# First norm of a one-layer encoder kernel taken from turned tokens, its first couple of weights in program order, and the rests of splits emitted one step later

## The chip, the cores and the metric

The kernel runs on one core of a Trainium2 chip. The metric is the time of one execution in microseconds (us) of the device, as a median of three runs; lower is better. TensorE (PE in the rows) multiplies matrices, VectorE (DVE) and ScalarE (ACT) work on elements, GpSimd (POOL) is hardly used, and the queue of SyncE (SP) issues all transfers.

## The reference, cut to what matters

```python
def swiglu(x, w_gate, w_up, w_down):
    return (silu(x @ w_gate) * (x @ w_up)) @ w_down

h = h + 0.5 * swiglu(rms_norm(h, norm_ffn1), ffn1_gate, ffn1_up, ffn1_down)
u = rms_norm(h, norm_mix)
xc, bg, cg, q, k, v, g_conv, g_attn = split(u @ w_in)
...                                   # gated convolution, differential attention, w_o
h = h + 0.5 * swiglu(rms_norm(h, norm_ffn2), ffn2_gate, ffn2_up, ffn2_down)
out = rms_norm(h, norm_final)
```

There are 1024 tokens of 1024 features; the hidden width of a swiglu is 2816. All is float32. `rms_norm` divides each token by the root of its mean square and multiplies by a gain for each feature.

## The kernel before, in words

**Layout.** Features lie on the 128 partitions and tokens along the row, so that x is `h[o][t]`: o is the half of the features (four blocks of 128), t the half of the tokens (512). A tile `Q` holds such a quarter, or 1 MB of weights; there are 19 of them. `C` is a tile of 128x512, `A` and `F` are tiles of 128x2x4x128 for stationary operands.

**Precision.** A float32 product is made of three matmuls of a rounded type: each operand is split into `hi`, a rounded copy made by ScalarE, and `lo = src - hi`, made by VectorE; then hi·hi, hi·lo and lo·hi are summed in PSUM. A group of one stationary tile and one quarter is 12 matmuls of 128x512.

**Fast product.** The weights of a swiglu come in pairs of 256 columns of gate and of up; the first pair is number 0. A product of a pair with x is a 2x2 product of blocks, done by seven products of sums of blocks (`ORDER`, `A_STEPS`, `B_STEPS`) in place of eight. The seven sums of quarters of x (`Blocks`, split into hi and lo) are made once and used by ten pairs; the sums of weights are made for each pair. A pair has 14 groups: seven of gate, seven of up. `submit` prepares a job's stationary operand, and runs the job four submits later. Pair 0 is done by eight plain products, since the seven sums aren't ready yet.

**Order.** Most of the program is ordered by a scheduler. The start (class `Start`) stands in the order of its code on TensorE, VectorE and ScalarE.

**The start before.** Pair 0 is multiplied with x times the gain, not yet divided by the root, in 16 groups; the results are multiplied with the root afterwards (`ev`). For the root, `squares` squares 16 tiles of 128x512 on ScalarE and VectorE adds them up (`add_square`); `norm` sums over partitions with a matmul against ones and makes the root in full width (`rstd`). `apply` then multiplies each quarter by gain and root in place, and the seven sums are made of that. The operands of the second half of the tokens are split twice: once without the root for pair 0 (`operand`), once with it for the later pairs.

**PSUM.** Tag `sc` has two buffers of 128x1024, `at` two, `ps` and `ot` one each of 128x512.

## Time and profile before

| | us |
|---|---|
| median of three runs | 2038.38 (2038.37 to 2039.26) |
| the profiled execution, its own time | 2041.61 |
| its span, first to last instruction | 2039.7 |
| TensorE busy | 1964.6 (96%) |
| VectorE busy | 1408.3 (69%) |
| ScalarE busy | 928.0 (45%) |
| mean granted clock of TensorE | 0.986 |

Busy TensorE of 96% says that over the whole span little is to be had anywhere but where TensorE waits. Such places are few: the first 100 us, and some stretches between 600 and 1450 us. In a row of a timeline, the number in square brackets is how long the engine was idle before it, with what ended that. A clock of 1.00 is 2.4 GHz, 0.50 is 1.2 GHz.

### The profile page before, as it was taken

How to read it: one execution, taken by the hardware profiler on the slowest of the kernel's cores; microseconds unless marked ns; L12 is line 12 of the kernel's file. 1: busy time of each engine (PE TensorE's matmuls, PEld its weight loads, DVE VectorE, ACT ScalarE, POOL GpSimd, SP SyncE). 2: the span in 40 equal slices, each digit the busy share in tenths (PEclk: the TensorE clock that was granted, in tenths of full speed). 3: DMA queues.
4: the chain of work that ended last, by engine and by line, in shares of the span. 5: the costliest groups of instructions: out<-in, count | busy, mean ns of one | idle time of the engine just before them, and what ended most of it. 6: DMA issues, size and time to landing. Idle time of an engine off the chain costs nothing.

```text
span 2039.7 us, 24072 instructions
## 1 busy us (share of the span) xinstructions
PE 1964.6 (96%) x8808; PEld 1617.4 (79%) x8808; DVE 1408.3 (69%) x2198; ACT 928.0 (45%) x1668; POOL 91.8 (4%) x91
## 2 busy tenths in 40 slices
PE   9799999999999999998999989999999999999997
PEld 7588888888887888886778867777788888888885
DVE  8976666666766755678576757988856656666874
ACT  6533333354355553233466645465433333353462
POOL 0000000000000000000344400000000000000000
PEclk9899999999999999999999999999999999999998
DMA  5132322345444332423424248032332232264341
GB/s 218 71 110 104 119 88 103 112 168 229 170 151 148 114 119 83 139 94 95 156 82 133 86 120 326 27 117 100 115 112 104 98 111 97 99 260 153 144 162 56
DMA packets 78582, 259.68 MB, mean 127 GB/s; under 512 B 9728, under 2 KB 16000, under 8 KB 60800
## 3 DMA queue, kind: packets, MB, share of 16 engines
q1 hardware_dynamic: 78464, 258.15, 35.3%
q8 instruction: 69, 1.13, 0.2%
q14 instruction: 49, 0.40, 0.1%
HBM read 183.14 MB, written 74.97 MB: 127 GB/s over the span
## 4 chain that ended last, share of the span: by engine, by line
PE 83%; DVE 11%; ACT 2%; issue 2%; DMA 1%; POOL 0%; SPq 0%; DVEq 0%; ACTq 0%; POOLq 0%
PE sc L273 37%; PE at L273 16%; PE ps L273 9%; PE ot L273 8%; DVE Q L249 3%; PE ps L1204 2%; PE sc L1265 1%; PE ps L1265 1%; DVE C L249 1%; DVE F L249 1%; PE at L1265 1%; PE sc L345 1%; PE sc L344 1%; PE sc L346 1%; PE sc L1000 1%
## 5 line engine op out<-in xcount | busy, mean ns | idle before, releaser
L273 PE MATMUL sc<-Q,A 128*128 128x512 f32 x2052 | 497.5, 392 | 13.8 <-DVE C L316 7.8
L273 PEld LDWEIGHTS sc<-Q,A 128*128 128x128 f32 x2052 | 388.2, 189 | 96.9 <-DVE C L316 8.1
L273 PE MATMUL sc<-Q,F 128*128 128x512 f32 x1488 | 362.6, 393 | 17.7 <-ACT Q L254 11.2
L273 PEld LDWEIGHTS sc<-Q,F 128*128 128x128 f32 x1488 | 281.7, 190 | 78.6 <-ACT Q L254 12.3
L249 DVE TENSOR_TENSOR F<-Q,F 128x512 fp32r<-128x512 f32 (+1 forms) x311 | 215.4, 697 | 170.9 <-ACT F L254 170.6
L249 DVE TENSOR_TENSOR Q<-Q,Q 128x512 fp32r<-128x512 f32 (+4 forms) x350 | 286.8, 873 | 34.4 <-ACT Q L254 27.1
L254 ACT CAST F<-Q 128x512 fp32r<-128x512 f32 (+1 forms) x319 | 193.7, 614 | 249.2 <-PE sc L273 88.5
L254 ACT CAST A<-Q 128x512 fp32r<-128x512 f32 (+1 forms) x303 | 183.9, 613 | 243.8 <-PE sc L273 100.9
L249 DVE TENSOR_TENSOR A<-Q,A 128x512 fp32r<-128x512 f32 (+1 forms) x303 | 205.1, 679 | 122.4 <-ACT A L254 121.7
L273 PE MATMUL at<-Q,F 128*128 128x512 f32 x1164 | 284.9, 391 | 4.8 <-DVE Q L405 3.0
L273 PEld LDWEIGHTS at<-Q,F 128*128 128x128 f32 x1164 | 219.4, 189 | 51.3 <-ACT Q L254 3.4
L254 ACT CAST Q<-Q 128x512 fp32r<-128x512 f32 (+1 forms) x214 | 153.1, 762 | 80.9 <-DVE Q L249 36.8
L249 DVE TENSOR_TENSOR C<-C,C 128x512 f32<-128x512 f32 x236 | 162.7, 693 | 16.9 <-ACT C L314 6.7
L249 DVE TENSOR_TENSOR Q<-Q 128x512 f32<-128x512 f32 x216 | 148.3, 691 | 2.4
L314 ACT COPY C<-sc 128x512 f32<-128x512 f32 x89 | 52.3, 588 | 149.0 <-PE sc L273 147.3
L273 PE MATMUL ps<-Q,A 128*128 128x512 f32 x474 | 118.3, 390 | 0.0
L1204 PE MATMUL ps<-Q,F 128*128 128x512 f32 x384 | 102.9, 403 | 4.3 <-ACT C L1210 4.2
L273 PE MATMUL ot<-Q,A 128*128 128x512 f32 x426 | 106.9, 392 | 0.0
L273 PEld LDWEIGHTS ps<-Q,A 128*128 128x128 f32 x474 | 89.3, 188 | 18.5
L273 PE MATMUL at<-Q,A 128*128 128x512 f32 x408 | 98.8, 389 | 0.0
L273 PE MATMUL ps<-Q,F 128*128 128x512 f32 x396 | 95.8, 389 | 0.0
L273 PEld LDWEIGHTS ot<-Q,A 128*128 128x128 f32 x426 | 81.0, 190 | 16.9
(214 smaller groups left out, 2069.1 us busy)
## 6 DMA issues: line engine op xcount, KB each, us to landing
Q<-in_ffn_gate SPq DMA_DIRECT2D x21, 1024.0 KB, 5.1
Q<-in_ffn_up SPq DMA_DIRECT2D x21, 1024.0 KB, 4.9
Q<-in_w_in SPq DMA_DIRECT2D x20, 1024.0 KB, 5.6
g1d<-C SPq DMA_DIRECT2D x77, 256.0 KB, 2.0
g2d<-C SPq DMA_DIRECT2D x77, 256.0 KB, 2.0
Q<-in_ffn_down SPq DMA_DIRECT2D x16, 1024.0 KB, 6.2
Q<-g1d SPq DMA_DIRECT2D x14, 1024.0 KB, 6.4
Q<-g2d SPq DMA_DIRECT2D x14, 1024.0 KB, 5.7
```

The lines of the kernel that those rows point to most:

```text
L249: e.tensor_tensor(out, a, b, op)
L254: self.nc.scalar.copy(hi, src)
L273: mm = lambda *x, **kw: self.nc.tensor.matmul(*x, skip_group_check=True, **kw)
L314: nc.scalar.copy(C[o, t], ps)
L344: mm(ps, a[:, 0, q], hi[:, q], start=n == q == 0, stop=False)
L345: mm(ps, a[:, 0, q], lo[:, q], start=False, stop=False)
L346: mm(ps, a[:, 1, q], hi[:, q], start=False, stop=n == 1 and q == 3)
L1000: nc.tensor.matmul(sc[:, a : a + w], qs[:, hl, s, qb * P : (qb + 1) * P], kst[:, s, a : a + w], start=hl == 0, stop=hl == 1 and a + w < n)
L1204: nc.tensor.matmul(ps, a[kk][:, x, q], y[:, q], start=c == 0, stop=c == 23)
L1265: self.k.nc.tensor.matmul(ps, a[:, x, kk], b[:, y, kk % 2], start=c == 0, stop=c == 11)
```

## The change

It has three parts.

1. The root of the first norm. `squares` turns 128 tokens at a time: eight transposes on TensorE put 128 tokens on partitions and 1024 features along the row of one `sc` buffer, and one ScalarE instruction squares the row and sums it. `root` makes the root of 4 columns with four VectorE instructions of 128x4, and puts it on the diagonals of four 128x128 blocks with four ScalarE instructions; `norm` spreads it over partitions by a matmul against ones and copies it to a tile. The root of the second half of the tokens (t = 1) is made first; `apply` then multiplies by gain and root and splits in one go, and what it makes for t = 1 serves pair 0 too (as sums 9 and 3), so that `operand` and the scaling in `ev` fall away for t = 1. The order of `run` is written anew around that.
2. Pair 1 (`ffn_in` with j from 1 to 2) is put in program order as well, and the loads of pair 2's weights stand at its 14th job in place of its third.
3. In `make_a` and in `Blocks`, the subtraction that makes `lo` is emitted one step after the copy that makes `hi`.

```diff
@@ Blocks.tiles
+        def rest(c):
+            k.tt(lo[:, c], self.q[x][t][:, c, :], hi[:, c].bitcast(F32), ALU.subtract)
...
-            k.split(self.q[x][t][:, c, :], hi[:, c], lo[:, c], key="b")
+            k.nc.scalar.copy(hi[:, c], self.q[x][t][:, c, :])
+
+            if c:
+                rest(c - 1)
+            if c == self.nk - 1:
+                rest(c)
@@ K.submit
             self.step()
+        while self.rests:
+            self.rests.pop(0)()
@@ K.make_a
-        self.split(get(*A_USE[i]), o[:, 0], o[:, 1], key="a")
+        src = get(*A_USE[i])
+        self.nc.scalar.copy(o[:, 0], src)
+        self.rests.append(lambda: self.tt(o[:, 1], src, o[:, 0].bitcast(F32), ALU.subtract))
@@ Start
+    def squares(self, t, b):
...
+        tp = k.ps("sc")
+        for o in range(2):
+            for j in range(4):
+                c = (4 * o + j) * P
+                nc.tensor.transpose(tp[:, c : c + P], self.h[o][t][:, j, b * P : (b + 1) * P], k.ident)
+        nc.scalar.activation(self.junk, tp, AF.Square, accum_out=self.w[t][:, 0, b : b + 1])
+
+    def root(self, t):
+
+        k, nc = self.k, self.k.nc
+        ss, y, v, a, r = (self.w[t][:, i] for i in range(5))
+        nc.scalar.activation(y, ss, AF.Abs_reciprocal_sqrt, bias=k.eps, scale=1.0 / D)
+        nc.vector.tensor_scalar(v, ss, 0.5 / D, 0.5 * EPS, ALU.mult, ALU.add)
+        nc.vector.tensor_tensor(a, y, y, ALU.mult)
+        nc.vector.tensor_tensor(v, a, v, ALU.mult)
+        nc.vector.scalar_tensor_tensor(r, v, -1.5, y, ALU.add, ALU.mult)
+        d = self.diag[t] = k.C()
+        for b in range(4):
+            nc.scalar.activation(d[:, b * P : (b + 1) * P], k.ident, AF.Copy, scale=r[:, b : b + 1])
 
     def norm(self, t):
+        ps = k.ps("sc")[:, :TH]
+        nc.tensor.matmul(ps, k.ones, self.diag[t], start=True, stop=True)
+        self.r[t] = k.C()
+        nc.scalar.copy(self.r[t], ps)
 
+    def apply(self, t, o, i):
+
+        self.B.left[i] = ()
+        for j, piece in enumerate(self.B.tiles(i)):
             u = self.h[o][t][:, j]
             self.k.nc.vector.scalar_tensor_tensor(u, u, self.gain(o, j, True), self.r[t], ALU.mult, ALU.mult)
+            piece()
+        if t == 1:
+            self.s[o, t] = self.B.made[i]
@@ Start.run, behind the first four groups
+        self.operand(1, 0, range(4))
+        self.weights(0, 0, 1)
+        self.squares(1, 0)
+        self.squares(1, 1)
+        self.mm(0, 0, 0, 1)
+        self.weights(0, 1, 1)
+        self.squares(1, 2)
+        self.squares(1, 3)
+        self.mm(0, 1, 0, 1)
+        self.root(1)
+        self.weights(1, 0, 1)
+        self.mm(1, 0, 0, 1)
+        self.norm(1)
+        self.weights(1, 1, 1)
+        self.apply(1, 0, 9)
+        self.mm(1, 1, 0, 1)
         self.squares(0, 0)
         self.squares(0, 1)
+        raws = load()
+        self.sc = k.ps("sc")
+        self.mm(0, 0, 1, 0)
+        self.squares(0, 2)
+        self.squares(0, 3)
+        self.apply(1, 1, 3)
+        self.root(0)
+        self.mm(0, 1, 1, 0)
+        self.norm(0)
         for x, o in XO:
+            self.ev(x, o, 0)
+        self.mm(0, 0, 1, 1)
+        self.mm(0, 1, 1, 1)
+        self.apply(0, 1, 2)
+        self.mm(1, 0, 1, 0)
+        self.mm(1, 1, 1, 0)
+        self.ev(0, 0, 1)
+        self.ev(0, 1, 1)
+        self.apply(0, 0, 1)
+        self.mm(1, 0, 1, 1)
+        self.mm(1, 1, 1, 1)
         self.B.plan(7)
+        self.ev(1, 0, 1)
+        self.ev(1, 1, 1)
@@ block_kernel, inside the stretch in program order
+        r = k.ffn_in(r, f.B, io["ffn1_gate"], io["ffn1_up"], g1d, 1, 2, 13)
+    k.ffn_in(r, f.B, io["ffn1_gate"], io["ffn1_up"], g1d, 2)
```

**What moves, at three places.** On ScalarE in the start, around the first norm, there stood splits of the second half's operands (`Q_117`, `Q_121`) and squares of 128x512 (L646), with the root in full width (L443) between them:

```order
L639 ACTIVATE Q_117<-Q_115,cst_85 128x512 x4
L646 ACTIVATE C_280<-Q_115 128x512
L646 ACTIVATE C_282<-Q_115 128x512
L646 ACTIVATE C_285<-Q_115 128x512
L646 ACTIVATE C_288<-Q_115 128x512
L443 ACT_TABLE_LOAD
L443 ACTIVATE C_292<-sc_124 128x512
L639 ACTIVATE Q_121<-Q_119,cst_85 128x512 x4
```

Now, from the copy of the second half's root (`C_324`) on, there are the hi of quarter (0, 1) (`Q_329`), four squares of turned blocks of the first half, the hi of quarter (1, 1) (`Q_413`), and the first half's root with its diagonals and its copy (`C_451`):

```order
L691 COPY C_324<-sc_322 128x512
L266 CAST A_326<-Q_101 128x512
L129 CAST Q_329<-Q_120 128x512 x4
L670 ACTIVATE Q_228,tn_355<-sc_356 128x1024
L670 ACTIVATE Q_228,tn_355<-sc_366 128x1024
L670 ACTIVATE Q_228,tn_355<-sc_393 128x1024
L670 ACTIVATE Q_228,tn_355<-sc_403 128x1024
L129 CAST Q_413<-Q_122 128x512 x4
L676 ACTIVATE tn_355<-tn_355,eps_89 128x4
L683 ACTIVATE C_432<-ident_93,tn_355 128x128 x4
L691 COPY C_451<-sc_449 128x512
```

So the hi of quarter (1, 1) stands behind all four squares, and the root behind that hi. On TensorE, pair 0's first two groups of the second half followed one another (`sc_124`, `sc_123`):

```order
L676 MATMUL sc_124<-Q_118,F_149 128x512
L676 MATMUL sc_124<-Q_117,F_149 128x512
L676 MATMUL sc_123<-Q_117,A_169 128x512
L676 MATMUL sc_123<-Q_118,A_169 128x512
L676 MATMUL sc_123<-Q_117,A_169 128x512 x2
```

Now transposes of two blocks of 128 tokens stand between them (`sc_380` holds both results; `sc_393` and `sc_403` hold turned blocks):

```order
L719 MATMUL sc_380<-Q_330,F_149 128x512
L719 MATMUL sc_380<-Q_329,F_149 128x512
L669 MATMUL sc_393<-ident_93,Q_102 128x128 x4
L669 MATMUL sc_393<-ident_93,Q_111 128x128 x4
L669 MATMUL sc_403<-ident_93,Q_102 128x128 x4
L669 MATMUL sc_403<-ident_93,Q_111 128x128 x4
L719 MATMUL sc_380<-Q_329,A_169 128x512
L719 MATMUL sc_380<-Q_330,A_169 128x512
```

The tile `sc_380` and the two turned blocks ask for three `sc` buffers, of which there are two. On VectorE in the projection `w_in`, near its end, the lo of a weight's sum (`F_6977`, `A_7009`) stood right behind the step that makes the sum:

```order
L967 TENSOR_TENSOR Q_6927<-Q_6823,Q_6927 64x512
L249 TENSOR_TENSOR Q_6565<-Q_6565 128x512
L249 TENSOR_TENSOR F_6977<-Q_6565,F_6977 128x512
L249 TENSOR_TENSOR Q_6565<-Q_6565 128x512
L316 TENSOR_TENSOR C_6947<-C_6947,at_6981 128x512
...
L967 TENSOR_TENSOR Q_6927<-Q_6823,Q_6927 64x512
L249 TENSOR_TENSOR Q_6619<-Q_6619 128x512
L249 TENSOR_TENSOR A_7009<-Q_6619,A_7009 128x512
L249 TENSOR_TENSOR Q_6619<-Q_6619 128x512
L316 TENSOR_TENSOR C_6969<-C_6969,sc_7013 128x512
```

Now the same lo (`F_7011`, `A_7043`) stand four or five rows later, and the second behind the addition that frees an `sc` buffer (L316 before, L330 now):

```order
L1014 TENSOR_TENSOR Q_6961<-Q_6857,Q_6961 64x512
L261 TENSOR_TENSOR Q_6599<-Q_6599 128x512 x2
L330 TENSOR_TENSOR C_6980<-C_6980,at_7014 128x512
...
L261 TENSOR_TENSOR F_7011<-Q_6599,F_7011 128x512
L1014 TENSOR_TENSOR Q_6961<-Q_6857,Q_6961 64x512
L261 TENSOR_TENSOR Q_6653<-Q_6653 128x512 x2
L330 TENSOR_TENSOR C_7002<-C_7002,sc_7046 128x512
L261 TENSOR_TENSOR A_7043<-Q_6653,A_7043 128x512
```

Apart from pairs 0 and 1 and from such swaps in the projection, no engine's order is changed, but for some neighbouring transfers that trade places and four matmuls.

## Rows read from the trace of the kernel before

**Rows 1.** Busy time in stretches: length, PE, PEld, DVE, ACT, POOL, PEclk, DMA share, GB/s.

```profile
60.00:80.00 20.00, 9.69 (x38) 7.18 (x38) 19.97 (x34) 9.90 (x16) 0.00 (x0) 0.83 0.17 66
120.00:160.00 40.00, 40.00 (x178) 33.14 (x177) 24.78 (x39) 15.85 (x29) 0.00 (x0) 1.00 0.31 112
```

**Rows 2.** Timeline of TensorE: start, length, line, operands, count, [idle before <-releaser].

```profile
18.34 2.88 PE L676 MATMUL ot<-Q,A 128*128 128x512 f32 x12
...
55.45 2.88 PE L273 MATMUL at<-Q,A 128*128 128x512 f32 x12
...
78.20 0.80 PE L273 MATMUL sc<-Q,F 128*128 128x512 f32 x1 [9.38 <-ACT Q L254]
...
81.21 0.79 PE L273 MATMUL sc<-Q,F 128*128 128x512 f32 x1 [1.79 <-ACT Q L254]
...
120.44 1.30 PE L273 MATMUL at<-Q,A 128*128 128x512 f32 x5
```

**Rows 3.** Timeline of VectorE in the first 120 us.

```profile
8.43 1.41 DVE L640 SCALAR_TENSOR_TENSOR Q<-Q,cst,Q 128x512 fp32r<-128x512 f32 x2 [5.66 <-ACT Q L639]
...
23.74 2.73 DVE L640 SCALAR_TENSOR_TENSOR Q<-Q,cst,Q 128x512 fp32r<-128x512 f32 x4
...
79.81 14.54 DVE L249 TENSOR_TENSOR Q<-Q,Q 128x512 f32<-128x512 f32 x24
...
113.62 0.69 DVE L249 TENSOR_TENSOR F<-Q,F 128x512 fp32r<-128x512 f32 x1 [0.61 <-ACT F L254]
```

**Rows 4.** Chain that ended last, in order of time: one group of 12 matmuls.

```profile
105.41 2.72 PE at L273 x12
```

**Rows 5.** Timeline of TensorE: four transposes in a row.

```profile
954.58 0.60 PE L974 MATMUL at<-ident,C 128*128 128x128 f32 x4
```

**Rows 6.** Timeline of TensorE: the first norm's matmul, in two passes.

```profile
23.78 1.02 PE L652 MATMUL sc<-C,ones 128*128 128x512 f32 x2
```

**Rows 7.** ScalarE's groups, shapes apart: count, busy us, mean ns, idle before.

```profile
L314 ACT COPY C<-sc 128x512 f32<-128x512 f32 x89 | 52.3, 588 | 149.0 <-PE sc L273 147.3 <-issue 1.7
...
L1018 ACT ACTIVATION_READ_ACCUMULATOR Q<-sc,sm 128x1 f32 x64 | 12.3, 192 | 0.0
...
L1018 ACT ACTIVATE Q<-sc,sm 128x1024 f32<-128x1024 f32 x8 | 8.9, 1118 | 0.3
...
L443 ACT ACT_TABLE_LOAD x5 | 6.4, 1283 | 1.2 <-PE ps L587 1.1
...
L254 ACT CAST A<-at 128x128 fp32r<-128x128 f32 x16 | 4.3, 267 | 8.2 <-DVE A L249 8.2
```

**Rows 8.** Timeline of ScalarE: four instructions of 128x512 in a row.

```profile
12.22 2.19 ACT L646 ACTIVATE C<-Q 128x512 f32<-128x512 f32 x4
```

**Rows 9.** VectorE's groups, shapes apart: a very small instruction.

```profile
L1025 DVE RECIPROCAL sm<-sm 128x1 f32<-128x1 f32 x32 | 5.0, 155 | 1.8 <-ACT Q L1018 1.8
```

**Rows 10.** Timeline of VectorE near the end of the projection.

```profile
953.71 0.69 DVE L249 TENSOR_TENSOR A<-Q,A 128x512 fp32r<-128x512 f32 x1 [0.69 <-ACT A L254]
...
964.26 0.69 DVE L249 TENSOR_TENSOR A<-Q,A 128x512 fp32r<-128x512 f32 x1 [0.69 <-ACT A L254]
...
965.47 0.68 DVE L316 TENSOR_TENSOR C<-C,sc 128x512 f32<-128x512 f32 x1
```

**Rows 11.** Timeline of TensorE at the same place.

```profile
966.20 5.16 PE L273 MATMUL sc<-Q,A 128*128 128x512 f32 x12 [7.83 <-DVE C L316]
```

**Rows 12.** Timeline of TensorE: a wait, and the matmuls behind it.

```profile
628.05 7.56 PE L273 MATMUL sc<-Q,F 128*128 128x512 f32 x22 [4.49 <-DVE Q L249]
```

**Rows 13.** Busy time in stretches: behind that wait, and within the attention.

```profile
628.00:630.00 2.00, 1.95 (x5) 1.59 (x6) 2.00 (x2) 0.00 (x0) 0.00 (x0) 0.50 0.00 0
...
1000.00:1100.00 100.00, 95.29 (x544) 80.70 (x543) 67.81 (x142) 66.77 (x177) 43.45 (x38) 1.00 0.33 105
```

**Rows 14.** The page's transfers: count, size, median us from issue to landing.

```profile
Q<-in_ffn_gate SPq DMA_DIRECT2D x21, 1024.0 KB, 5.1
```

**Rows 15.** Transfers of the first 60 us: count, size, median us from issue to landing.

```profile
Q<-in_ffn_gate SPq DMA_DIRECT2D x2, 1024.0 KB, 8.7
```

More of the change, by code (lines that the diff above doesn't have):

```diff
@@ L179, in __init__ @@
         self.slow = deque()
+        self.rests = []
         self.rot = self.na = 0
@@ L470, in setup, with ffn_in @@
         nc.vector.tensor_scalar(self.ng, self.cst[:, 0:32], -1.0, None, ALU.mult)
+        self.ident = self.t("ident", [P, P])
+        make_identity(nc, self.ident)
     def ffn_loads(self, wg, wu):
         return [self.load_raw(wg[0]), self.load_raw(wu[0])]
-    def ffn_in(self, raws, B, wg, wu, gd, j0=0):
+    def ffn_in(self, raws, B, wg, wu, gd, j0=0, j1=NFP, at=2):
         nc = self.nc
-        for j in range(j0, NFP):
+        for j in range(j0, j1):
             rg, ru = raws
@@ L502, in ffn_in @@
             for n, (p, r) in enumerate(jobs):
-                if n == 2 and j + 1 < NFP:
+                if n == at and j + 1 < NFP:
                     raws = [self.load_raw(wg[j + 1]), self.load_raw(wu[j + 1])]
                 self.submit(p, r)
+        return raws
     def finished(self, G, o, t, gd, j):
@@ L607, in __init__ @@
         raws = [k.t("Q", [P, 2, 8, P]) for _ in range(2)]
[L608 removed]
+        self.w, self.diag, self.r, self.s, self.A, self.acc, self.G = {}, {}, {}, {}, {}, {}, {}
         self.B = Blocks(k, 4)
@@ L640, in operand @@
             nc.vector.scalar_tensor_tensor(lo[:, j], src, self.gain(o, j), hi[:, j].bitcast(F32), ALU.mult, ALU.subtract)
-    def squares(self, o, t):
+    def squares(self, t, b):
         k, nc = self.k, self.k.nc
-        for j in range(4):
-            sq = k.C()
-            nc.scalar.activation(sq, self.h[o][t][:, j], AF.Square)
-            k.add_square(self.st, t, sq)
+        if (t, b) == (1, 0):
+            self.junk = k.t("Q", [P, D])
+        if b == 0:
+            self.w[t] = k.t("tn", [P, 5, 4], bufs=2)
+        tp = k.ps("sc")
[15 more added lines that the diff above has]
+            nc.scalar.activation(d[:, b * P : (b + 1) * P], k.ident, AF.Copy, scale=r[:, b : b + 1])
     def norm(self, t):
         k, nc = self.k, self.k.nc
-        ps = self.sc[1][:, :TH] if t == 0 else k.ps("at")
-        nc.tensor.matmul(ps, k.ones, self.st[t][0], start=True, stop=True)
-        self.r[t] = k.rstd(ps, D, TH)
-    def apply(self, t, o):
-        for j in range(4):
+        ps = k.ps("sc")[:, :TH]
[5 more added lines that the diff above has]
+        for j, piece in enumerate(self.B.tiles(i)):
             u = self.h[o][t][:, j]
             self.k.nc.vector.scalar_tensor_tensor(u, u, self.gain(o, j, True), self.r[t], ALU.mult, ALU.mult)
+            piece()
+        if t == 1:
+            self.s[o, t] = self.B.made[i]
     def weights(self, x, o, kk):
@@ L679, in ev @@
         k, nc = self.k, self.k.nc
-        c = k.C()
-        nc.vector.scalar_tensor_tensor(c, self.acc.pop((x, o)), -1.0, self.r[t], ALU.mult, ALU.mult)
+        c = self.acc.pop((x, o, t))
+        if t == 0:
+            ps, c = c, k.C()
+            nc.vector.scalar_tensor_tensor(c, ps, -1.0, self.r[t], ALU.mult, ALU.mult)
         if x == 0:
-            nc.scalar.activation(c, c, AF.Silu)
-            self.G[o, t] = c
+            g = self.G[o, t] = c if t == 0 else k.C()
+            nc.scalar.activation(g, c, AF.Silu)
         else:
@@ L692, in run @@
         XO = [(0, 0), (0, 1), (1, 0), (1, 1)]
-        B = self.B.get
-        self.sc = [k.ps("sc"), k.ps("sc")]
+        warm = k.ps("sc")
         for _ in range(self.WARM):
-            k.nc.tensor.matmul(self.sc[0][:, :P], k.ones, k.ones, start=True, stop=True)
+            k.nc.tensor.matmul(warm[:, :P], k.ones, k.ones, start=True, stop=True)
         self.operand(0, 0, (0, 1))
@@ L704, in run @@
             self.mm(x, o, 0, 0)
-        self.squares(0, 0)
-        self.operand(1, 0, range(4))
-        for o in range(2):
-            self.weights(0, o, 1)
-        self.mm(0, 0, 0, 1)
-        self.squares(1, 0)
-        for o in range(2):
-            self.weights(1, o, 1)
-        self.operand(0, 1, range(4))
-        self.squares(0, 1)
-        self.norm(0)
-        self.mm(0, 1, 0, 1)
-        self.operand(1, 1, range(4))
-        self.squares(1, 1)
-        raws = load()
-        self.mm(1, 0, 0, 1)
-        self.ev(0, 0, 0)
-        self.ev(0, 1, 0)
-        self.mm(1, 1, 0, 1)
-        self.ev(1, 0, 0)
-        self.ev(1, 1, 0)
-        for x, o in XO[:2]:
-            self.mm(x, o, 1, 0)
-        self.apply(0, 0)
-        self.norm(1)
-        for x, o in XO[2:]:
-            self.mm(x, o, 1, 0)
-        B(1)
-        self.apply(0, 1)
-        self.mm(*XO[0], 1, 1)
-        B(2)
-        for x, o in XO[1:]:
-            self.mm(x, o, 1, 1)
-        self.apply(1, 1)
-        for x, o in XO:
-            self.ev(x, o, 1)
-        self.apply(1, 0)
+        self.operand(1, 0, range(4))
[14 more added lines that the diff above has]
+        self.mm(1, 1, 0, 1)
+        self.squares(0, 0)
+        self.squares(0, 1)
+        raws = load()
[6 more added lines that the diff above has]
+        self.mm(0, 1, 1, 0)
+        self.norm(0)
+        for x, o in XO:
+            self.ev(x, o, 0)
[9 more added lines that the diff above has]
+        self.mm(1, 1, 1, 1)
         self.B.plan(7)
+        self.ev(1, 0, 1)
+        self.ev(1, 1, 1)
         return raws
@@ L781, in constants @@
         k, nc = self.k, self.k.nc
-        self.ident = k.t("ident", [P, P])
-        make_identity(nc, self.ident)
+        self.ident = k.ident
         mm = k.C()
```

13 lines of the change are left out of this document (5 added, 8 removed).

## The prediction

> **What bounds the kernel now.** I read the busy time by stretches first, then the timelines of TensorE and VectorE in the first 120 us, then the waits of TensorE elsewhere. From 120 us on TensorE is busy without a gap at the full clock; between 60 and 80 us it is busy for 9.69 of 20 us, and VectorE for 19.97 [rows 1]. On TensorE pair 0 ends without a stall; pair 1's first group stands at 55.45, and then come waits, 9.38 the longest, behind ScalarE's hi of sum 7, whose source VectorE delivers [rows 2]. VectorE has its first wait since 8.43 at 113.62 [rows 3]. So the start is bound by VectorE, and the rest of the kernel mostly by TensorE.
>
> How much the start costs: a group takes 2.72 us [rows 4], 0.2267 per matmul. In program order 211 matmuls of pairs 1 and 2 stand ahead of the row at 120.44 [rows 2]. Back to back they are 47.8 us, so TensorE stands as if pair 1 had begun at 120.44 - 47.8 = **72.6 us** and never waited. That number is what the change can move. Pair 0 ends near 55.2 (0.2 before the row at 55.45, whose weights load first), so 17.4 us are lost there, part of them at half clock.
>
> **Prices.** VectorE at 128x512: 0.602 per instruction in a row (14.54 less a tail of 0.09, over 24), 0.66 with a gain (2.73 less 0.09, over 4), 0.69 until the result is there [rows 3]. ScalarE at 128x512: 0.52 in a row [rows 8], about 0.62 until the result. A group 2.72 [rows 4]; a transpose 0.11 in a row (0.60 less the last one's 0.27, over three) [rows 5]; the norm's matmul 0.87 (1.02 [rows 6] less the 0.16 by which a group's 2.88 [rows 2] outlasts 2.72; bound above 1.02). A square of a turned block was not there before: the nearest is the attention's exponential of 128x1024 from PSUM with a sum, 1.12 and 0.19 for the sum [rows 7]; I take 1.13 from one to the next and 1.3 until the sum, bounds 1.02 and 1.31. Table load 1.28, four diagonals about 0.9 (0.27 each until the result, bounds 0.8 and 1.1), copy from PSUM 0.59 [rows 7]. A root instruction of 128x4: 0.16 [rows 9].
>
> **What part 1 removes.** From VectorE: 14 additions of squares (8.4), six instructions of the wide roots (3.6), eight lo with gain (5.3), four scalings (2.4), less four lo for sum 9 (2.4) and the eight tiny ones (1.3): about 16 us. If VectorE stayed busy throughout, the start would gain most of that. It doesn't.
>
> **What part 1 makes wait.** I walk the three queues from the fourth group's end at 21.06 (18.34 + 2.72 [rows 2]), each instruction at the latest of its queue and its sources, with 0.04 for a hand-over.
>
> - TensorE turns two blocks (1.8), does a group (25.5), turns two more (27.3), does a group (30.0). ScalarE squares the last of these blocks until 29.1, loads the table until 30.2, and after the root (0.2), four tiny instructions (30.9) and four diagonals (31.8) casts the next weights at 32.4. TensorE waits 2.5, and 0.3 for the lo: 35.5.
> - The norm's matmul (36.4), its copy, then the cast behind it in ScalarE's queue (37.6): TensorE waits 1.3 and 0.3, group to 40.7, two turned blocks to 42.4.
> - VectorE, which sat idle 8.3, 3.4, 1.2, 1.6 and 4.6 so far, applies and splits quarter (0, 1) until 43.6. ScalarE squares the first half's blocks behind its four hi: 42.9 to 45.3. The next group's `sc` buffer is free when the first square ends: TensorE waits 1.8, and is done at 47.0.
> - One block turned (47.9). The other needs the same buffer, hence the square of the first (48.1 to 49.4): turned at 50.3, TensorE idle 1.6. Group to 53.0. Last square 50.5 to 51.8.
> - Only now come quarter (1, 1)'s hi in ScalarE's queue. VectorE stands at its first lo from 45.0 to 52.3: 7.3 idle. Done at 56.2; root 56.8; diagonals 57.8; TensorE, idle 4.9, starts the norm's matmul at 57.9; copy at 59.5. VectorE idle 2.7, first `ev` at **59.6**.
>
> VectorE's waits sum to 29.6 us with 0.5 of short ones, against 16 saved. From 59.6 it is the bound again. In the new order 88 instructions stand from that `ev` to the lo of pair 2's second gate group (6 of `ev`, 16 of two quarters, 6 of pair 0's end, then 60): pair 1's lo now stand between the splits of its sums, by program order, where before they were done before sum 7. The first 87 cost 79 x 0.603 + 8 x 0.663 = 52.9, and 4.5 of waits: thirteen times a lo stands two rows behind its sum or so and waits 0.17 (0.69 + 0.62 + 0.08 against 1.20), two lo of weights right behind theirs 0.79 each, and 0.74 go for pair 0's last group. So that lo is started at 117.0 and there at 117.7. Of its group ten matmuls are left (2.3), and with one group more fourteen groups of pairs 1 and 2 are done at 122.7. Fourteen groups are 38.1: TensorE stands as if pair 1 had begun at **84.7**, 12.1 later than before. The 64 transposes (7 us) lie inside these waits, and so does pair 0, which ends at 58.75 + 6 x 2.72 = 75.1.
>
> **The clock.** After a wait of 4.49 the clock stood at 0.50 [rows 13], and 22 matmuls took 7.56 where 5.0 + 0.16 are due: 2.4 lost [rows 12]. The same after 7.83, 12 matmuls in 5.16 [rows 11]. The new wait of 4.9 should do that; pair 0's end, at which VectorE waits, moves by it: **+2.4**, bounds 0 and 2.6.
>
> **Part 2** moves pair 2's loads to the 14th job. The program gives them the buffers of quarters (1, 0) and (1, 1), free when VectorE has split sums 4 and 5, at about 107 and 113.5 in this walk. At 5.1 to landing [rows 14] they are there at 112.2 and 118.6, against casts wanted at about 115 and 122. I cost it at nothing; the cover is 3 us each.
>
> **Part 3** in the projection: VectorE waits 0.69 for ScalarE's hi three times (two stand in the rows) in the last 12 us before the addition that frees an `sc` buffer [rows 10], and TensorE waits 7.83 for that [rows 11]. With the lo some rows later these waits go (2.1), the last lo stands behind the addition (0.6), and one lo enters the stretch from ahead (0.6 the other way); with some tenths of another such wait: **-2.4**, bounds 0 and -3.4. The clock falls in what is left of the wait, as before. Elsewhere a lo has four jobs' lead, and TensorE doesn't wait.
>
> **Sum.** 12.1 + 2.4 - 2.4 = **+12.1 us** on the profiled execution, 2041.61 to 2053.7. That execution is 3.2 above the median of the runs, so 2038.4 + 12.1 = **2050.5**.
>
> **Rivals.** (a) *Faster*: ScalarE's queue does not hold up VectorE. If the four squares and hi pass each other so that the last three long waits (4.6, 7.3, 2.7) go, 14.6 and the clock's 2.4 are gained: 2033.5. It speaks for it that VectorE alone bounds the start now; against it that the order of each queue is fixed, and that hi (1, 1) stands behind squares which need a buffer that the group before them keeps. It decides from where VectorE's waits fall below 29.6 - 12.1 = 17.5. Chance 0.10. (b) Waits near that point, a wash at 2034 to 2042: 0.06. (c) The transposes don't hold the clock: from 40.7 TensorE does only transposes and waits until 44.3, and the group there at half clock takes 2.4 more, which the chain behind it hands on: 2052.9. The clock among the attention's transposes is 1.00, but matmuls lie between them [rows 13]. Chance 0.15.
>
> The Trainium skill, page "TensorE: Matmul & The Clock Gate", section "Part 4: PE-mode transpose", says of TensorE's transposes that they don't count as busy in the same way for the clock; by that rule (c) would be the case, and no row here has transposes alone.
>
> (d) Pair 2's weights land late: 8.7 us to landing, as the first 60 us have it [rows 15], instead of 5.1 adds 1 to 3: 2053. Chance 0.10. (e) Part 3 does nothing, since the stretch waits for transfers instead: 2052.9. Chance 0.10. The forecast has 0.49, with 2046 to 2055 as its own range.
>
> **Range and chances.** The unknown prices: squares' bounds move the sum by -0.6 and +0.9 (six in the chain); transposes at 0.27 would add up to 8, but the row of four in 0.60 stands near 0.11. With (c) to (e) on top the range goes to 2057; downward, the clock not falling, part 3 at its bound and two or three us of the walk's waits, and half of (b), make 2041. 0.2% is about what a measurement of this kernel can tell from no change, 4.1 us. Faster by more than that 0.10, within it 0.06, slower 0.84.
>
> **What would show it.** The timeline of VectorE: a wait of about 7 us before a lo of quarter (1, 1) near 45 to 52, and the first `ev` near 60. TensorE: a wait of 4 to 5 us before the second norm's matmul near 58, pair 0's end at 75 to 78, a clock of 0.50 behind; 211 matmuls of pairs 1 and 2 done some 12 to 15 us later than 120.4. In the projection: the wait of 7.83 down to some 5.4. The forecast is wrong if VectorE's waits before its first `ev` sum to less than 20 us, or if the stretch behind 130 us gains or loses more than 4 us.

## The result and the profile after

| | before | after |
|---|---|---|
| median, first series | 2038.82 us (4 runs) | 2060.05 us (4 runs, 2057.93 to 2061.52) |
| median, second series | 2039.42 us (10 runs) | 2058.31 us (5 runs, 2053.44 to 2062.93) |
| spans of the profiled executions | 2039.7, 2039.5, 2039.3 | 2056.1, 2060.9, 2059.3, 2060.6 |
| VectorE busy (first profile) | 1408.3 us | 1394.0 us |

The changed kernel is slower: ratio 1.0098 [1.0085, 1.0111], then 1.0091 [1.0077, 1.0104]. VectorE works 14.3 us less and the kernel takes about 20 more. The sign was forecast, the size was not: 2050.5 was named, and 2057 as the upper end.

The first view is the busy time by stretches in the changed kernel (columns as in [rows 1]):

```profile
120.00:160.00 40.00, 39.55 (x175) 32.45 (x174) 31.36 (x52) 17.86 (x31) 0.00 (x0) 1.00 0.57 209
60.00:80.00 20.00, 19.82 (x75) 15.52 (x76) 14.96 (x23) 11.20 (x19) 0.00 (x0) 0.87 0.07 26
```

Between 60 and 80 us TensorE is now busy throughout, where it was for 9.69 [rows 1]: but with pair 0, which before had ended at 55. From 120 us on it is again nearly without a gap. The timeline of TensorE in the start, after:

```profile
32.98 4.69 PE L719 MATMUL ps<-Q,F 128*128 128x512 f32 x12 [2.88 <-ACT F L266]
...
39.92 3.31 PE L719 MATMUL ot<-Q,A 128*128 128x512 f32 x12 [1.19 <-ACT A L266]
43.06 1.91 PE L669 MATMUL sc<-ident,Q 128*128 128x128 f32 x16
46.28 3.02 PE L719 MATMUL sc<-Q,F 128*128 128x512 f32 x12 [1.31 <-ACT Q L670]
...
51.44 1.09 PE L669 MATMUL sc<-ident,Q 128*128 128x128 f32 x8 [1.27 <-ACT Q L670]
...
60.18 2.07 PE L689 MATMUL sc<-C,ones 128*128 128x512 f32 x2 [4.90 <-ACT C L683]
61.27 5.20 PE L719 MATMUL sc<-Q,F 128*128 128x512 f32 x12
...
79.93 0.61 PE L287 MATMUL sc<-Q,F 128*128 128x512 f32 x2
84.25 3.43 PE L287 MATMUL sc<-Q,F 128*128 128x512 f32 x10 [3.71 <-DVE F L261]
87.48 3.69 PE L287 MATMUL at<-Q,A 128*128 128x512 f32 x12
...
123.21 5.28 PE L287 MATMUL sc<-Q,F 128*128 128x512 f32 x22 [0.45 <-DVE F L261]
```

The reader is to see two things. The waits stand where the walk of the queues put them (2.5, 1.3, 1.8, 1.6 and 4.9 were forecast; 2.88, 1.19, 1.31, 1.27 and 4.90 stand here). But a group of twelve takes 4.69 behind the first of them, 5.20 behind the 4.90, and 3.43 + 3.69 for 22 matmuls behind the 3.71, where 2.72 and 5.0 are due (and 0.16 more for the last matmul of a row). The granted clock in stretches says why; it is the column before the last two:

```profile
33.00:37.00 4.00, 4.00 (x11) 2.92 (x12) 0.65 (x1) 0.00 (x0) 0.00 (x0) 0.69 0.00 0
...
46.20:49.00 2.80, 2.72 (x12) 2.26 (x13) 1.07 (x2) 1.15 (x3) 0.00 (x0) 1.00 0.01 3
...
60.10:62.00 1.90, 1.82 (x3) 0.84 (x3) 0.00 (x0) 0.03 (x1) 0.00 (x0) 0.50 0.00 0
...
84.00:88.00 4.00, 3.75 (x12) 2.97 (x13) 3.92 (x8) 1.30 (x3) 0.00 (x0) 0.72 0.27 106
```

The timeline of VectorE, after:

```profile
24.82 0.69 DVE L261 TENSOR_TENSOR A<-Q,A 128x512 fp32r<-128x512 f32 x1 [7.71 <-ACT A L266]
28.88 0.17 DVE L677 TENSOR_SCALAR tn<-tn 128x4 f32<-128x4 f32 x1 [3.37 <-ACT Q L670]
...
39.90 0.69 DVE L261 TENSOR_TENSOR A<-Q,A 128x512 fp32r<-128x512 f32 x1 [6.25 <-ACT A L266]
...
54.29 0.69 DVE L261 TENSOR_TENSOR Q<-Q,Q 128x512 fp32r<-128x512 f32 x1 [7.02 <-ACT Q L129]
...
62.91 1.29 DVE L726 SCALAR_TENSOR_TENSOR C<-at,C 128x512 f32<-128x512 f32 x2 [4.10 <-ACT C L691]
80.13 0.69 DVE L261 TENSOR_TENSOR C<-C,ps 128x512 f32<-128x512 f32 x1 [1.83 <-PE ps L719]
121.86 1.29 DVE L261 TENSOR_TENSOR F<-Q,F 128x512 fp32r<-128x512 f32 x2
```

With the waits of 1.44 and 1.91 between them, VectorE stands for 31.8 us before its first `ev` at 62.91 (29.6 and 59.6 were forecast). Two later waits of TensorE, at the place of 4.49 before [rows 12] and, in the projection, of 7.83 before [rows 11]:

```profile
645.68 6.82 PE L287 MATMUL sc<-Q,F 128*128 128x512 f32 x22 [4.48 <-DVE Q L261]
979.71 4.59 PE L287 MATMUL sc<-Q,A 128*128 128x512 f32 x12 [4.42 <-DVE C L330]
```

These two rows stand in every kernel below. Their starts, called the first and the second mark, cut its span into three: the start shifts the first mark, part 3 shortens the way to the second, and the rest should be the same for all.

| kernel | first mark | to the second | from there to the span's end |
|---|---|---|---|
| before, 3 profiles | 627.5 to 628.1 | 337.9 to 338.2 | 1073.5 to 1073.9 |
| after, 4 profiles | 644.2 to 646.2 | 334.0 to 335.2 | 1076.4 to 1081.4 |
| mean difference | +17.4 | -3.2 | +5.5 |

### The profile page after: what moved, and what is told of

The parts are those of the page before. It is cut to its first block, busy times and chain, and to the rows that moved or that the text cites. A ratio compares the mean times of both kernels' runs of the same rounds, so it can differ in the third digit from the quotient of the medians.

```text
span 2056.1 us, 24166 instructions
## 1 busy us (share of the span) xinstructions
PE 1978.4 (96%) x8872; PEld 1624.3 (79%) x8872; DVE 1394.0 (68%) x2178; ACT 925.3 (45%) x1672; POOL 90.9 (4%) x91
## 4 chain that ended last, share of the span: by engine, by line
PE 84%; DVE 9%; ACT 3%; issue 2%; DMA 1%; SPq 0%; POOL 0%; DVEq 0%; ACTq 0%; POOLq 0%
PE sc L287 36%; PE at L287 16%; PE ps L287 9%; PE ot L287 7%; DVE Q L261 4%; PE ps L1251 2%; PE sc L1312 1%; PE ps L1312 1%; PE at L1312 1%; PE sc L1047 1%; PE sc L360 1%; PE sc L359 1%; PE sc L358 1%; DVE F L261 1%; PE ot L1123 1%
## 5 line engine op out<-in xcount | busy, mean ns | idle before, releaser
L280 ACT CAST F<-Q 128x512 fp32r<-128x512 f32 (+1 forms) x287 | 173.9, 611 | 246.6 <-PE sc L287 80.1
L280 ACT CAST A<-Q 128x512 fp32r<-128x512 f32 (+1 forms) x287 | 173.5, 611 | 221.0 <-PE sc L287 86.6
L261 DVE TENSOR_TENSOR C<-C,C 128x512 f32<-128x512 f32 x222 | 152.5, 690 | 15.6 <-ACT C L328 6.7
L266 ACT CAST Q<-Q 128x1024 fp32r<-128x1024 f32 (+1 forms) x94 | 83.9, 938 | 38.9 <-DMA Q<-g1d 14.4
L330 DVE TENSOR_TENSOR C<-C,sc 128x512 f32<-128x512 f32 x82 | 56.2, 685 | 57.0 <-PE sc L287 38.7
```

The lines of the kernel that those rows point to most:

```text
L261: e.tensor_tensor(out, a, b, op)
L266: self.nc.scalar.copy(hi, src)
L280: self.nc.scalar.copy(o[:, 0], src)
L330: nc.vector.tensor_tensor(C[o, t], C[o, t], ps, ALU.add)
```

## The experiments

**Part 3 alone, and all but part 3.** The kernel before with the three hunks of part 3 (`Blocks.tiles`, `submit`, `make_a`), and the changed kernel with the first and the last of these undone (`submit` then has nothing to run). The hunk of `make_a`:

```diff
-        self.split(get(*A_USE[i]), o[:, 0], o[:, 1], key="a")
+        src = get(*A_USE[i])
+        self.nc.scalar.copy(o[:, 0], src)
+        self.rests.append(lambda: self.tt(o[:, 1], src, o[:, 0].bitcast(F32), ALU.subtract))
```

> The kernel before with part 3 alone (the lo of sums of weights and of sums of x one step later); the start's own code is untouched. The trace of the changed kernel has its wait in the projection down from 7.83 to 4.42 and the twelve matmuls behind it from 5.16 to 4.59. Theory A, the loss is all in the start and part 3 only gains: pair 1 still stands as if begun near 72.6, the wait in the projection near 4.4, and the time is 2038.8 less 4 = 2034.8 (2033 to 2036.5). Theory B, the deferred lo also costs what was lost between 1230 and 1400 us (waits of 3.99 and 2.75 where 2.55 and 1.82 stood, about 3 us in all with the matmuls behind them): 2038 (2037 to 2040).

> The changed kernel without part 3: every lo right behind its hi again, also in pair 1, which stands in program order. Theory A, part 3 is a plain gain of some 4 in the projection and nothing in the start: 2060 + 4 = 2064 (2062.5 to 2066). Theory C, part 3 also carries the start, as in program order a lo right behind its hi waits 0.69 where it now waits 0.17 or nothing: 24 pieces of sums of x and of pair 1's weights at 0.5 to 0.6 more each are 12 to 14 more, so 2073 to 2080. Theory B, part 3 costs 3 between 1230 and 1400 us: 2061.

Part 3 alone takes 2037.15 us against 2040.1, ratio 0.9984 [0.9975, 0.9993]: faster than both kernels. Its TensorE in the projection:

```profile
960.91 4.59 PE L287 MATMUL sc<-Q,A 128*128 128x512 f32 x12 [4.97 <-DVE C L330]
```

First mark 626.3, 334.6 to the second, 1072.5 behind it, and waits of 2.70 and 1.88 where theory B had 3.99 and 2.75: by the trace theory A, nothing lost later. The time lies outside its 2033 to 2036.5, as the kernel before took 2040.1 in this series and the gain is 3.0, not 4; the trace is of the fastest of eleven executions (2035.32). Without part 3 the changed kernel takes 2085.97, 26 to 28 more than with it, and not 4: theory C, at twice its price. Its VectorE, in the timeline, waits for ScalarE's hi at nearly every lo:

```profile
41.59 0.69 DVE L252 TENSOR_TENSOR Q<-Q,Q 128x512 fp32r<-128x512 f32 x1 [0.69 <-ACT Q L257]
...
59.23 0.69 DVE L252 TENSOR_TENSOR Q<-Q,Q 128x512 fp32r<-128x512 f32 x1 [10.16 <-ACT Q L257]
...
120.34 1.29 DVE L252 TENSOR_TENSOR Q<-Q,Q 128x512 fp32r<-128x512 f32 x2 [0.69 <-ACT Q L257]
```

Between 40 and 150 us there are 36 such waits of about 0.69, 25 us in sum, where the changed kernel has 2; its first mark is at 671.2, 26 later.

**Half of part 3.** Only the lo of sums of weights one step later.

> The kernel before with the lo of sums of weights one step later, and the lo of sums of x where they were: half of part 3. Theory A, the gain in the projection comes from the lo of weights, which stood behind their hi in the last 12 us before the addition that frees TensorE: the wait there is near 4.4 to 5 as with both halves, and the time 2037 to 2038 against 2040 of the kernel before. Rival, both halves are needed, or the half for x brings it: the wait stays at 7.8 and the time at 2040.

2038.07 against 2039.77, ratio 0.9989 [0.9980, 0.9998]; the projection's wait is 5.39, the way to the second mark 335.1 (338.0 before, 334.6 with both halves). Wait and time lie just outside theory A's bounds, but most of the gain is the weights' half.

**The clock in the start.** Matmuls of zeros, which add nothing to open sums, fill TensorE's first, second and longest wait:

```diff
+    def fill(self, x, o, t, hi, n):
+        for _ in range(n):
+            self.k.nc.tensor.matmul(self.acc[x, o, t], self.k.zero, hi, start=False, stop=False)
@@ run, ahead of the groups (1, 0, 0, 1) and (1, 1, 0, 1), and of the second norm
+        self.fill(1, 0, 0, self.s[1, 0][0][:, 0], 10)
+        self.fill(1, 1, 0, self.s[1, 0][0][:, 0], 3)
+        self.fill(0, 1, 1, self.s[0, 1][0][:, 0], 18)
```

> The changed kernel with 10, 3 and 18 matmuls of zeros, which add nothing to open sums, in TensorE's waits of 2.88, 1.19 and 4.90 us in the start. Theory A, the clock that falls in these waits costs the start time (the groups behind them took 4.69, 3.31 and 2.07 + 5.20 where 2.72 and 0.87 + 2.72 are due): these groups go back to about 2.75, the first evaluation on VectorE moves from 62.9 to about 59.5, and the time falls by 3 to 4, to 2056.5 (2055.5 to 2058). Rival, VectorE alone sets the start behind its long wait and the slow groups only use up slack: 2060 (2059 to 2061).

2052.56 us, 5.8 to 7.5 below the changed kernel's medians, where theory A had 3 to 4. Its timelines of TensorE and VectorE:

```profile
32.13 3.29 PE L725 MATMUL ps<-Q,F 128*128 128x512 f32 x12 [0.56 <-ACT F L266]
...
57.78 1.12 PE L691 MATMUL sc<-C,ones 128*128 128x512 f32 x2 [0.83 <-ACT C L685]
58.34 3.30 PE L725 MATMUL sc<-Q,F 128*128 128x512 f32 x12
...
118.34 5.28 PE L287 MATMUL sc<-Q,F 128*128 128x512 f32 x22 [0.45 <-DVE F L261]
```

```profile
59.56 1.29 DVE L732 SCALAR_TENSOR_TENSOR C<-at,C 128x512 f32<-128x512 f32 x2 [3.15 <-ACT C L693]
```

The groups take full-clock times again, the first `ev` comes 3.35 earlier, the row of 22 4.87 earlier (0.8 of each is the input x arriving earlier in this execution, by VectorE's row at 24.82, here 24.04). The first mark is at 640.8, 4.3 below the mean of the changed kernel, again with the 0.8. So the clock in these three waits costs 3.5 to 4.1 in the start, and VectorE hands it on. What the time fell beyond that stands behind the second mark, at 1074.2.

**The order of ScalarE's queue.** First all four squares of the first half ahead, with the root ahead of quarter (1, 1); the transposes and the norm's matmul move with them on TensorE. Then, on top, the casts of pair 0's last two weights ahead of the second half's root (a third move, of `weights(0, 1, 1)` ahead of a group, changes no engine's order):

```diff
-        self.squares(0, 0)
-        self.squares(0, 1)
+        for b in range(4):
+            self.squares(0, b)
         raws = load()
         self.sc = k.ps("sc")
         self.mm(0, 0, 1, 0)
-        self.squares(0, 2)
-        self.squares(0, 3)
-        self.apply(1, 1, 3)
         self.root(0)
-        self.mm(0, 1, 1, 0)
+        self.apply(1, 1, 3)
         self.norm(0)
+        self.mm(0, 1, 1, 0)
```

```diff
         self.squares(1, 1)
+        self.weights(0, 1, 1)
         self.mm(0, 0, 0, 1)
-        self.weights(0, 1, 1)
         self.squares(1, 2)
         self.squares(1, 3)
-        self.mm(0, 1, 0, 1)
-        self.root(1)
         self.weights(1, 0, 1)
+        self.weights(1, 1, 1)
+        self.mm(0, 1, 0, 1)
+        self.root(1)
         self.mm(1, 0, 0, 1)
         self.norm(1)
-        self.weights(1, 1, 1)
```

> The changed kernel with all four squares of the first half ahead of pair 0's fifth group of the second half's kind, and the root ahead of the split of quarter (1, 1), so that no square needs the buffer which the group in between keeps, and the hi of quarter (1, 1) no longer holds up the root. Theory A, the start is late since ScalarE's queue and the two sc buffers hold up VectorE (waits of 7.02 and 4.10): these two waits shrink to 2 to 4 together, the first evaluation comes near 54, and the time falls by 7 to 9, to 2052 (2050.5 to 2054). Rival, VectorE's wait only moves, to the four squares in a row and to pair 0's end on TensorE: 2058 to 2060.

> The kernel with all four squares of the first half ahead (2046.5), and on top of it the casts of pair 0's last two weights ahead of the second half's root in ScalarE's queue, and so ahead of its copy; nothing else. Theory A, the new order lets ScalarE's queue hold up both other engines: TensorE's waits of 2.88 and 1.19 in front of these groups go, and with them the clock's fall (another 2.5); VectorE's waits of 1.91 and 6.24 go too, its first product with the root comes near 35 where it came near 41, the whole start ends 6 to 10 earlier, and the time is 2038 (2036 to 2041). Rival, the two casts only push the root back and the wait moves to the root's matmul: 2044 to 2047.

The first takes 2046.48, below theory A's range. Its first `ev`:

```profile
56.09 1.28 DVE L726 SCALAR_TENSOR_TENSOR C<-at,C 128x512 f32<-128x512 f32 x2
```

It was expected near 54. The first mark stands at 637.4, 7.7 below the changed kernel's mean and within the 7 to 9 of theory A, and behind the second mark it takes 1073.4, where the rest of the gain lies. The second has its first mark at 633.4, another 4.0 lower where 6 to 10 were expected: TensorE's waits of 2.88 and 1.19 are gone and VectorE's first product with the root is at 34.81 in place of 40.17, but a wait of VectorE came back behind that, and on TensorE the clock fell in a new place, behind sixteen transposes in 1.91 and a wait: the next sixteen took 3.50, at a granted clock of 0.61 and then 0.50.

```profile
45.33 0.17 DVE L677 TENSOR_SCALAR tn<-tn 128x4 f32<-128x4 f32 x1 [5.08 <-ACT Q L670]
```

```profile
36.76 1.91 PE L669 MATMUL sc<-ident,Q 128*128 128x128 f32 x16
40.59 3.50 PE L669 MATMUL sc<-ident,Q 128*128 128x128 f32 x16 [1.92 <-ACT Q L670]
```

Its time, 2045.77, shows only 0.7 of the 4.0; behind the second mark it takes 1077.4. So the order of ScalarE's queue, with what moves along on TensorE, is worth 11.7 in the start. The first mark still stands 5.7 behind the kernel before, though part 2 gains in this start (next experiment).

**Part 2 undone.** Pair 1 outside the stretch in program order, with pair 2's loads at its third job, in the changed kernel and in the one with squares and weights ahead:

```diff
-        r = k.ffn_in(r, f.B, io["ffn1_gate"], io["ffn1_up"], g1d, 1, 2, 13)
-    k.ffn_in(r, f.B, io["ffn1_gate"], io["ffn1_up"], g1d, 2)
+    k.ffn_in(r, f.B, io["ffn1_gate"], io["ffn1_up"], g1d, 1)
```

> The changed kernel with pair 1 outside the stretch in program order (part 2 undone: the scheduler orders it, and pair 2's loads stand at its third job). Theory A, the first half's late root costs nearly all, and VectorE is the bound from there, so the order of pair 1 matters little: within 2 of the changed kernel, 2058 to 2062. Rival, program order keeps the first lo of pair 1 behind all of pair 0's end (TensorE waits 3.71 and then runs 24 matmuls 1.7 too slowly): 5 faster, 2055. A third, the loads of pair 2 were put late for a reason, and earlier ones hold buffers that the sums want: slower, above 2063.

> The kernel with the squares and the weights ahead, and pair 1 outside the stretch in program order. If pair 1's program order costs the wait of 3.71 and the clock behind it, this is 5 below the kernel with squares and weights ahead, near 2033, and below both kernels; if VectorE is the bound there, it is within 2 of it, near 2038.

2064.52 and 2051.09: 6.2 and 5.3 above their counterparts. For the second, near 2033 or near 2038 was expected; both answers fell. TensorE in the first of them:

```profile
106.28 8.37 PE L287 MATMUL sc<-Q,F 128*128 128x512 f32 x24 [12.59 <-ACT C L328]
```

The wait of 3.71 is gone, and one of 12.59 stands for it: the third answer held in sign and size, though its reason (buffers) isn't shown. Part 2 gains 5 to 6 of the time; by the first mark, which stands at 650.9 and 641.4, it gains 5.7 and 8.0 in the start. Loads issued earlier within the program order were not tried: the buffers that they take are free only then.

**Turned blocks in the old order.** The start of the kernel before (first half's root first, `ev` and quarters as VectorE comes to them, pair 1 left to the scheduler) with part 3 and of part 1 only the root by turned blocks; then the same with two scalings and the first quarter's `apply` ahead of the second half's root in VectorE's queue:

```diff
-        self.squares(0, 0)
+        self.turn(0, 0)
+        self.turn(0, 1)
...
+        self.square(0, 0)
+        self.square(0, 1)
...
+        self.root(0)
         self.mm(0, 0, 0, 1)
+        self.norm(0)
```

```diff
+        c = [self.scaled(0, o, 0) for o in range(2)]
         self.weights(1, 1, 1)
         raws = load()
+        self.apply(0, 0)
...
         self.root(1)
-        self.ev(0, 0, 0)
-        self.ev(0, 1, 0)
+        for o in range(2):
+            self.ev(0, o, 0, c[o])
```

> The order of the kernel before in the start (root of the first half first, evaluations of pair 0 filling VectorE, pair 1 left to the scheduler), part 3, and of part 1 only the way the root is made: turned blocks squared and summed by ScalarE, small roots and diagonals. Operands and the scaling for the second half stay as before. Theory A, the squares by turned blocks are no loss in themselves, only their place in ScalarE's queue was: VectorE loses 14 additions and six wide root instructions (12.0 at 0.60), gains eight tiny ones (1.3), TensorE gains 64 transposes and later root matmuls (7 to 8) ahead of pair 1, where it now loses 17: pair 1 stands as if begun 4 to 8 earlier than in the kernel with part 3 alone (2037.2), so 2031 (2028.5 to 2034). Rival, the transposes and their buffers hold up TensorE and ScalarE here too, and the start ends later: 2038 to 2045.

> The kernel with turned blocks in the old order (2044.6), with VectorE's work that needs only the first half's root (two scalings of pair 0, the first quarter times gain and root) ahead of the second half's root in VectorE's queue; ScalarE's Silu stay behind that root, so that no table is loaded twice more. Theory A, the saved instructions of VectorE come back as waits (16 us of them before its first scaling at 39.67), and what can be put into these waits is gained: the scalings start near 33 in place of 39.7 and the start ends 4 to 5 earlier, 2040 (2037.5 to 2042). Rival, something else than VectorE's waits sets the start there (TensorE's 64 transposes ahead of pair 1): 2044 to 2045.

The first takes 2044.63, ratio 1.0014 [1.0005, 1.0023], the second 2041.29, 1.0004 [0.9995, 1.0013]. Theory A of the first fell: its first mark is at 630.8, 4.6 behind part 3 alone. VectorE's 10.7 saved (the estimate above) came back as 14.9 of waits before its first scaling at 39.67 (36.29 in the kernel before). The second filled part of them (first scaling at 33.13) and has its mark at 628.0, about that of the kernel before. But both have part 3, so the kernel to compare with is part 3 alone (626.3, 2037.15): with the best place found here, turned blocks are still 1.8 later than wide squares by the mark and some 4 in the time.

**A plain delay.** Part 3 alone, and 86, 20 or 38 matmuls of zeros in a group of pair 3:

```diff
@@ in a group, behind each step's first matmul
+            self.count += 1
+            if self.count == 150:
+                for _ in range(86):
+                    mm(ps, self.zero, hi[:, k], start=False, stop=False)
```

> The kernel with part 3 alone (2037.2) and 86 matmuls of zeros, 19.5 us at 0.2267, inside one group of pair 3, where TensorE is busy without a gap: the start's loss without the new start. It adds nothing to the sums. Theory A, the start's delay is all that the changed kernel pays, and what is left (2058 to 2060 against 2037.2 + 19.4 = 2056.6, with single runs from 2053.4 to 2062.9) is the clock behind later waits, which any shift of the later stages can change: the median here lies at 2056.7 or up to 3 above it, with a spread like the changed kernel's. Rival, the changed kernel pays something of its own behind the start: exactly 2056.7 within 1 here, with a spread as small as that of the kernel with part 3 alone (3 us).

> The kernel with part 3 alone and 20 matmuls of zeros (4.5 us) inside a group of pair 3: the same instructions behind it, only later. Behind the projection's wait the kernel with part 3 alone took 1072.5 and with 86 such matmuls 1071.7, while the kernel with turned blocks in the old order, whose instructions stand in the same order there, took 1077.3. Theory A, the moment at which the waits come decides whether the clock falls behind them: some shift by a few us alone moves this stretch to 1075 to 1077 (time 2037.2 + 4.5 + 3 to 5 = 2045 to 2047). Rival, the shift alone does nothing: 1072 to 1073, and 2041.7.

> As the run with 20 matmuls of zeros, with 38 (8.6 us). Theory A, the moment decides: here or in the run with 20 the stretch behind the projection's wait takes 1075 to 1077 in place of 1072.5, and the time is 3 to 5 above 2037.2 + 8.6 = 2045.8. Rival, a shift alone does nothing: 1072 to 1073 and 2045.8.

2055.97, 2042.18 and 2045.92, against 2056.7, 2041.7 and 2045.8 by the plain sum: by the medians the rivals hold, and a shift costs its length. Behind the second mark their single profiles take 1071.7, 1075.8 and 1073.9. The 1075.8 lies where theory A had it, and of the nine runs with 38 two took 2050.88 and 2051.65; but single runs of the kernel before spread from 2038.13 to 2044.45 too, so that it isn't shown that the shift does this. With 86 the first mark is at 647.4, 2.3 behind the changed kernel's mean, and the time is 2.3 to 4.1 below its medians: the changed kernel pays something of its own behind the start.

**The same kernels again.** The changed kernel three times more, the kernel before twice, each with a profile; the numbers stand in the first two tables.

> The changed kernel once more, unchanged, to see how far its own executions lie apart. The four runs so far lie 21.2 above the kernel before in the median, the profiled one only 16.3 above the profiled one of before. Theory A, what is left over (about 5) is the clock's behaviour after the many short waits behind 600 us, which differs from one execution to the next: the runs spread over 3 to 5 us, the median is 2058 to 2061, and in this profile the stretch from the wait of 2.97 near 1330 to the wait of 4.27 near 1396 takes 64.2 as in four other profiles and not 65.8. Rival, the change costs a fixed 1.5 there: 65.8 again.

> The changed kernel, unchanged, for a third profile. Its first two took 415.9 and 420.9 from the end of the projection's wait to the wait of 4.27 near 1396, where the kernel before took 412.7. Theory A, the changed kernel's stretch is longer on average only through the clock that falls or not behind waits that stand in both kernels: 412 to 421, with the granted clock of some 20 us pieces at 0.83 or 0.91 in the long ones. Theory B: always above 415, the waits themselves longer.

> The kernel before, unchanged, for a second profile of it. Theory A: from the end of the projection's wait (966.20 in its first profile) to the wait of 4.26 near 1379 it takes 412 to 414 as in the first, and the rest 660 to 661. Theory B, the stretch varies as much here as in the changed kernel: up to 417.

Behind the second mark the three profiles of the kernel before keep to 0.4 us, as theory A had it, and the four of the changed one to 5. From the second mark to the wait of 4.27 near 1396 the latter take 415.9 to 420.9, in the range of theory A and all above 415, as theory B had it; both of B's longer waits are there too (3.31 to 3.99 where 2.45 to 2.65 stood, 2.75 where 1.82 to 1.87 stood). The two theories aren't told apart by this. The busy time by stretches of the changed kernel, in its first and in its second profile, each 20 us long and 20 us behind the second mark:

```profile
999.71:1019.71 20.00, 17.17 (x84) 13.94 (x83) 12.99 (x27) 9.63 (x25) 8.02 (x8) 1.00 0.39 127
```

```profile
999.48:1019.48 20.00, 17.38 (x70) 14.17 (x69) 11.84 (x26) 6.96 (x18) 6.34 (x7) 0.83 0.30 99
```

The same program does 84 matmuls at full clock in one, 70 at 0.83 in the other; in both the stretch holds the same wait of 2.62, and in the second the clock falls behind it. Farther on, all four profiles of the changed kernel have 65.8 between the waits of 2.97 and 4.27 (near 1330 and 1396), all three of the kernel before 64.2: theory A's 64.2 fell, the rival's 65.8 stands. The rows of the changed kernel there, and those of the kernel before:

```profile
1329.82 3.01 PE L287 MATMUL at<-Q,F 128*128 128x512 f32 x12 [2.97 <-DVE Q L419]
...
1351.69 6.42 PE L287 MATMUL at<-Q,F 128*128 128x512 f32 x20 [2.75 <-DVE F L261]
```

```profile
1314.68 4.58 PE L273 MATMUL at<-Q,F 128*128 128x512 f32 x12 [2.97 <-DVE Q L405]
...
1336.56 4.85 PE L273 MATMUL at<-Q,F 128*128 128x512 f32 x20 [1.82 <-DVE F L249]
```

In the changed kernel the clock holds behind the first wait, TensorE is through earlier and waits longer for VectorE, and the clock falls behind that second wait, where nothing hides it. All twenty profiles of this document pass the place in one of these two ways. In seven the clock holds first and 65.8 are taken: the four of the changed kernel, and the kernels with the weights ahead, with the weights ahead and pair 1 scheduled, and with turned blocks in the old order (the first of the two). In thirteen it falls first and 64.2 are taken, among them the filled kernel and the one with the squares ahead. So these 1.6 are no fixed price of the new start.

## Why the prediction was wrong in size

- **What bounds, and which way.** Right: VectorE, relieved of 14 us (about 16 were counted), stands for 31.8 before its first `ev`. That it had no wait before from 8.43 to 113.62 was misread by one of 0.24 at 39.01, which changes nothing. The long wait stands at the lo of quarter (1, 1) behind four squares, as walked, and moving the squares takes 7.7 back.
- **The walk, +12.1.** Right within 1.3 at the clock that it assumed. With the waits filled, the first `ev` comes at 59.56 (59.6 walked) and TensorE stands as if pair 1 had begun at 118.34 - 146 x 0.2267 = 85.2 (84.7 walked; 85.2 + 0.8 - 84.7 = 1.3 short, as x came 0.8 earlier in that execution). Pair 0 ends there at 72.36 + 2.72 = 75.1, as walked. That these agree so closely is partly luck, by the same 0.8. Of the single prices, four diagonals took 1.28 in a row, not 0.9.
- **The clock, +2.4: the step that failed.** It counted one fall, behind the wait of 4.9. The rows have three (behind 2.88, 4.90 and 3.71), and the first two, with what VectorE hands on, are 3.5 to 4.1 by the kernel with the waits filled; the bound of 2.6 was too low. The third stands in that kernel too and isn't priced. The wait of 3.71 was not in the walk: the lo of pair 1's first weights stand behind pair 0's end on VectorE. The same place in the changed kernel is 90.1 (123.21 - 146 x 0.2267), so the start lost 17.5 by its own yardstick and 17.4 by the first mark, where 14.5 was forecast; the clock explains 1.1 to 1.7 of these 3, the walk's own shortfall the rest.
- **Part 2 at nothing.** Right for the loads: they are issued at 112.41 and 118.80, ScalarE's cast waits 1.66 for the second, and TensorE has no wait behind 123.21 up to the first mark. That program order itself was worth 5 to 6 of the time, against a scheduled pair 1, no step said.
- **Part 3, -2.4.** -3.2, within its bounds. What it does in the start was inside the walk and not told apart: without it this start is 26 later.
- **Nothing elsewhere: the second step that failed.** "Elsewhere ... TensorE doesn't wait" left out that it does, in both kernels, and that the clock may fall behind those waits. Behind the second mark the changed kernel pays 5.5 on the mean of four profiles, where nothing was forecast. Some 3 of that stand in all four: at least 84.6 where 83.1 stood from the norm near 1245 to the wait of 2.97, and 65.8 where 64.2 stood behind it; both stand in some of the other kernels too. The rest differs from one execution of the same program to the next (1076.4 to 1081.4), so it isn't work. By the medians a shift alone doesn't do it. What decides in which wait the clock falls stays open.
- **Profiled execution against median.** 3.2 was taken off, since the profiled execution of the kernel before lay above its median. The changed kernel's four profiled spans lie at 2059.2 on the mean, 19.7 above those of before (17.4 - 3.2 + 5.5), its medians 18.9 and 21.2 above.
- **Rival (c), the clock among transposes.** It didn't come true in this kernel. From 43.06 TensorE has transposes and a wait of 1.31 only, and the group at 46.28 takes 3.02 at 1.00. The Trainium skill, page "TensorE: Matmul & The Clock Gate", section "Part 4: PE-mode transpose", says that transposes don't count as busy in the same way; by that rule, as the prediction reads it, this group would have run at half clock, and the trace doesn't agree. The rule isn't refuted by that: with the weights ahead the clock fell behind transposes and a wait of 1.92, so that it stays open whether transposes count. Rivals (a) and (b) fell with the sign; (d) cost nothing; (e) is refuted by part 3 alone.

## What to carry to other kernels

Work taken off the engine that bounds a stage is worth only what that engine then does earlier: here 14 us of VectorE came back as 31.8 of waits behind ScalarE's queue, which is seen by walking the queues, not by summing busy times. A new wait of TensorE is priced with the matmuls behind it at half clock too, where rows behind waits of like length show that, and every wait of the walk is asked, not the longest alone. Emitting a dependent subtraction one step later cost nothing, was worth 3 us by itself, and 26 where the order is fixed by hand: it is the version that beats both kernels.
